# Hybrid decoder layer: late products by tile, and GpSimd's loads and sums behind copies

## The chip, the cores and the metric

The kernel runs on one core of one Trainium2 chip. The metric is the device time of one execution in microseconds (us); the number given for a kernel is the median of its runs.

## The reference

One decoder layer on 512 tokens with 16 learned meta tokens ahead (528 positions, 1024 channels), in float32:

```python
u = rmsnorm(h, mix_norm_w)
proj = u @ w_in                      # u_pool | z | xbc | dt | gates
gates = sigmoid(proj[..., OFF_GATE:] + b_gate)
y_pool = pool_mixer(u_pool, pool_w_group, pool_scale) @ w_pool_up
y_ssd = mamba2_branch(z, xbc, dt_raw, ...) @ w_ssd_out   # 8 groups, chunks of 128
h = h + (gate_pool * y_pool + gate_ssd * y_ssd) @ w_o
v = rmsnorm(h, mlp_norm_w)
hid = relu(v @ w_ff1)
h = h + (hid * hid) @ w_ff2
out = rmsnorm(h, final_norm_w)[:, N_META:]
```

`mamba2_branch` convolves xbc, scans chunk by chunk, adds a skip term, multiplies with silu(z) and normalizes each of the eight groups of 256 channels. `pool_mixer` takes running means over 2, 4, 8 and 16 positions in four groups and mixes each with a 256x256 matrix.

## The kernel before

Activations stand channels by tokens, 128 channels to a tile. Each float32 product is made of three matmuls of a faster type: a factor is cast to a high half (ScalarE: `whi`, `shi`, `yh`) and the rest is a low half (VectorE: `wlo`, `slo`, `yl`), and PE multiplies high by high, high by low and low by high. Many products are seven half-size ones in Strassen's way instead of eight; their factors need sums of quarters of the weights.

The stages follow each other: projections and scan of the groups 0 to 7, woven together; during the last group's scan, which has no projection beside it, `out_part` multiplies the scan's outputs with w_ssd_out; then the pool stage (`pool_pair`, `pool_mix`, and between them the last products of w_ssd_out, tiles psl); then the merge (`gate_ssd`, tiles pgs, and products with w_pool_up, tiles pup; the gates multiply, sums go to acc); then w_o (tiles wo_alpha, wo_q, wo_p); then the MLP, whose first layer's products (pf, px) run between those of the second (alpha, q, p).

**out_part.** The y of groups 0 to 6 are the 14 pairs `ys[0]` to `ys[13]`; this function uses 8 to 13. For the first two output tiles (psp0, psp1) it does `ys[8..11]` first, then, when the y of group 6 are there, the late products with `ys[12]` and `ys[13]`; then the six other tiles. Each tile is copied from PSUM by ScalarE (`add`, tile sp) and added to `acc_d` in DRAM by a GpSimd DMA. The PSUM pool psa has two buffers, so tile n + 2 waits for the copy of tile n. `ssd` of group 7 runs at the same time; at its end it makes the last y (`ys[14]`, `ys[15]`).

**Gates.** Seven pool gates lie in DRAM (`gate_d`) since the scan and are loaded into `m1[d]` by GpSimd DMAs in the pool stage; the eighth is written directly.

**Weight sums.** For each set of quarters in `sets`, `weight_sums` issues four (w_ff2) or eight (w_in, w_ff1) GpSimd DMAs of 512 KB that copy quarters from DRAM to DRAM and accumulate; the issuing queue waits where one step reads what another wrote. There are 15 sets, 11 of them are made in the scan, each step behind a copy of a column by GpSimd into `seen`, which makes it wait for its place. The remaining four are made at the end of the merge, behind the loads of `ht` (the residual), which wait until the memory of u is free:

```python
for t in range(4):
    ht_load = nc.gpsimd.dma_start(ht[:, t, :], x[t * P : (t + 1) * P, :])
while sets:
    with tc.issue_after(ht_load.ins):
        ht_load = weight_sums()
```

Weights come in blocks of 128 x 1024 (512 KB), loaded by SyncE into three `raw` buffers (`block_load`, L95); a load waits until VectorE has made the low half from the block before in that buffer. There are four buffers each for the halves.

The order of an engine's instructions is set by a scheduler from the order of the code and from estimates; `tc.issue_after(i)` puts an instruction behind another in its engine's order, `tc.high_priority` moves it ahead where its operands allow it. A DMA that stands behind a copy in GpSimd's queue waits for what that copy waits for.

Of the kernel before, what the change touches and what calls it, by code (L numbers as in the profile page):

```python
# [9 lines left out]
F32 = mybir.dt.float32  # L10
F32R = mybir.dt.float32r
AF = mybir.ActivationFunctionType
ALU = mybir.AluOpType

P = 128
# [37 lines left out]

SETS_AT = {0: 1, 1: 1, 2: 2, 3: 1, 4: 2, 5: 2, 6: 1, 7: 1}
PIECES = {4: 21, 7: 14}
SETS_POOL = 0

PLAIN = 4

# [5 lines left out]
def kernel(ctx: ExitStack, tc, xT, x, w, fx, f1, f2, vec, fnw, out):  # L65
# [100 lines left out]
    def col(off, i, n=P):  # L166
        return vs[:n, off + i : off + i + 1]
# [426 lines left out]
    def ssd(g, cur):  # L594
# [121 lines left out]
        for c in range(4):  # L716
            dve.reciprocal(rs[:, ctok(c)], rs[:, ctok(c)])
        yield
        for i in range(2):
            y = yt[:, i, :]  # L720
            dve.scalar_tensor_tensor(y, y, col(V_SN, 2 * g + i), rs, op0=ALU.mult, op1=ALU.mult)
            yh = yp.tile([P, SEQ], F32R, tag="yh", name=f"yh{g}_{i}")
            yl = yp.tile([P, SEQ], F32R, tag="yl", name=f"yl{g}_{i}")
            act.copy(yh, y)
            dve.tensor_tensor(yl, y, yh.bitcast(F32), op=ALU.subtract)
            ys.append((yh, yl))
        yield

    late_cast, last_state = [None], {}
# [112 lines left out]
    def out_part():  # L842

        def get(n):
            t = block_tiles()
            block_load(t, slice(0, 1024))

            with after(b_meta[G - 1] if n == 1 else None):
                cast = act.copy(t[2], t[1])
            if n == 1:  # L850
                late_cast[0] = cast
            with tc.issue_after(x_decayed[G - 1].ins) if n == 1 else nullcontext():
                dve.tensor_tensor(t[3], t[1], t[2].bitcast(F32), op=ALU.subtract)
            return t

        def pieces():
            blocks = [get(0), get(1)]
            for n in range(6):
                t = blocks[n] if n < 2 else get(n)
                for j in range(NK):  # L860
                    c = slice(j * P, (j + 1) * P)
                    yield t[2][:, c], t[3][:, c]

        un = pieces()

        def part(ps, d, ks):
            mm3s(ps, [(next(un), ys[k]) for k in ks], ks[0] == 8, ks[-1] == 13)

        def add(ps, d):
            o = staged(f"sp{d}")  # L870
            act.copy(o, ps)
            nc.gpsimd.dma_start(acc_d[d], o, accum_op=ALU.add)


        ps = [psum2(f"psp{d}")[:, :SEQ] for d in range(2)]
        for d in range(2):
            part(ps[d], d, range(8, 12))
            yield
        late = [[(next(un), ys[k]) for k in (12, 13)] for d in range(2)]
        for o in ((0, 0), (1, 0), (0, 1)):  # L880
            for d in range(2):
                for n, (a, b) in enumerate(late[d]):
                    pe.matmul(ps[d], a[o[0]], b[o[1]], start=False, stop=o[1] == 1 and n == 1)
            yield
        for d in range(2):
            add(ps[d], d)
        for d in range(2, NK):
            ps = psum2(f"psp{d}")[:, :SEQ]
            part(ps, d, range(8, 14))
            add(ps, d)  # L890
            yield
# [162 lines left out]

    for d in range(NK):
        t_load = nc.gpsimd.dma_start(acc[d], acc_d[d])
    for _ in range(SETS_POOL):
        with tc.issue_after(t_load.ins):
            t_load = weight_sums()
    pend = [pooled_halves(*a) for a in pool_pair(POOL_ORDER[0])]  # L1060

    un = units()
# [11 lines left out]
    for n in range(1, 4):  # L1074
        pend, ahead = nxt, None
        if n < 3:
            nxt, ahead = pool_pair(POOL_ORDER[n + 1]), POOL_ORDER[n + 1]
        if n == 2:
            wgb = block()
        else:  # L1080
            gts.append(gate_ssd(MERGE[len(gts)]))

        pend = [pooled_halves(*a, copied.get(ahead)) for a in pend]
        with tc.issue_after(last[ahead].ins) if n < 3 else nullcontext():
            pool_mix(POOL_ORDER[n], pend, wgb)
        if n == 1:
            for d in MERGE:
                with tc.issue_after(mixed[0].ins):
                    if d < NK - 1:
                        nc.gpsimd.dma_start(m1[d], gate_d[d])  # L1090
    pool_stack.close()
# [82 lines left out]
    for n, d in enumerate(MERGE):  # L1174

        with ExitStack() as st:
            if n == 1:
                for i in mixed:
                    st.enter_context(tc.issue_after(i.ins))
            if 0 < n < NK - 1:  # L1180
                gts.append(gate_ssd(MERGE[n + 1]))
        if n >= NK - 2:
            first.append(split(woq["b11", n - NK + 2]))
        ps = psum2(f"pup{d}")[:, :SEQ]
        wh, wl = block()
        if n < len(WO_ORDER):
            wo_load(*WO_ORDER[n])
        cs = [slice(k * P, (k + 1) * P) for k in ks]
        mm3s(ps, [((wh[:, c], wl[:, c]), yps[k]) for c, k in zip(cs, ks)])
        dve.tensor_tensor(acc[d], acc[d], gts[n], op=ALU.mult)  # L1190
        dve.tensor_tensor(m1[d], m1[d], ps, op=ALU.mult)
        dve.tensor_tensor(acc[d], acc[d], m1[d], op=ALU.add)
        factors(d)
# [652 lines left out]
```

## Time and profile before

| | |
|---|---|
| median of 3 runs | 1000.05 us (999.04 to 1002.26) |
| the profiled execution | 1001.71 us, span of its profile 1000.0 us |
| busy, share of the span | PE 99%, weight loads of PE 87%, DVE 80%, ACT 60%, POOL 12% |
| clock granted to TensorE | 0.998 |
| DMA | 184.52 MB, mean 185 GB/s |

PE is TensorE, PEld its weight loads, DVE VectorE, ACT ScalarE, POOL GpSimd, SP SyncE. In a timeline a row has the start in us, the busy time, the engine, the line, the operation, output<-inputs by tile names, shapes, the count, and in brackets the idle time before it with what ended it. Where one row holds several instructions, the busy time is that of all. Lines are those of the kernel before.

### The profile page before, as it was taken

The page shows a single profiled execution, that of the slowest core. Times are in us where ns is not written, and L with a number is a line of the kernel's source. Part 1 is how long each engine was busy: PE and PEld are TensorE (multiplying, and loading weights), DVE is VectorE, ACT ScalarE, POOL GpSimd, SP SyncE. Part 2 cuts the span into 40 slices and gives each one's busy share as a digit, 9 for nine tenths or more (in the row PEclk, how much of TensorE's full clock was granted, in tenths as well). Part 3 has the DMA queues.
Part 4 walks back from the last instruction along what each step waited for, and adds up shares of the span by engine and source line. Part 5 has one row for each costly group of instructions (what it writes and reads, how often), then busy time and mean ns, then how long its engine had stood idle before and what let it go on. Part 6 is the DMA issues. An engine that isn't in the chain of part 4 may idle for free.

```text
span 1000.0 us, 15672 instructions
## 1 busy us (share of the span) xinstructions
PE 987.8 (99%) x6035; PEld 873.8 (87%) x6035; DVE 803.9 (80%) x1162; ACT 602.2 (60%) x855; POOL 119.5 (12%) x215
## 2 busy tenths in 40 slices
PE   9999999999999999999999999999999999999997
PEld 7889998989889999978898888888789999999986
DVE  7978997879845888988789666975988888888885
ACT  7657839495924658574345433477666656656654
POOL 0011321211212212223200001121000000000000
PEclk9999999999999999999999999999999999999999
DMA  7284968666798848768723723899354454454332
GB/s 261 78 254 149 268 197 214 190 191 212 230 271 235 245 129 259 226 163 171 271 85 127 253 85 112 228 243 314 92 190 148 148 190 144 152 186 150 129 106 85
DMA packets 61803, 184.52 MB, mean 185 GB/s; under 512 B 7072, under 2 KB 8416, under 8 KB 60704
## 3 DMA queue, kind: packets, MB, share of 16 engines
q1 hardware_dynamic: 39456, 109.00, 32.7%
q0 software_dynamic: 18240, 67.51, 26.4%
q10 hardware_dynamic: 4032, 7.00, 1.9%
q8 instruction: 47, 0.77, 0.3%
q14 instruction: 28, 0.23, 0.1%
HBM read 173.13 MB, written 58.59 MB: 232 GB/s over the span
## 4 chain that ended last, share of the span: by engine, by line
PE 93%; ACT 3%; DVE 2%; DMA 1%; issue 0%; SPq 0%; ACTq 0%; DVEq 0%
PE px L1465 8%; PE px L215 8%; PE alpha L1533 6%; PE pz L215 6%; PE px L1468 4%; PE px L218 4%; PE alpha L1536 3%; PE pgp L215 3%; PE pz L218 3%; PE pgs L215 3%; PE py L694 2%; PE pqx L509 2%; PE pso L146 1%; PE pgp L218 1%; PE wo_alpha L1226 1%; PE po L688 1%
## 5 line engine op out<-in xcount | busy, mean ns | idle before, releaser
L113 DVE TENSOR_TENSOR wlo<-raw,whi 128x1024 fp32r<-128x1024 f32 (+2 forms) x88 | 102.0, 1171 | 46.8 <-ACT whi L111 31.0
L111 ACT CAST whi<-raw 128x1024 fp32r<-128x1024 f32 (+2 forms) x88 | 87.2, 1011 | 70.3 <-PE pso L147 15.3
L215 PE MATMUL px<-uh,whi 128*128 128x264 f32 (+1 forms) x320 | 80.9, 291 | 0.0
L218 PE MATMUL px<-ul,whi 128*128 128x264 f32 (+1 forms) x320 | 78.8, 285 | 0.0
L1240 DVE TENSOR_TENSOR ht<-ht,alpha 128x1024 f32<-128x1024 f32 x35 | 42.7, 1220 | 29.1 <-PE alpha L1533 29.1
L215 PEld LDWEIGHTS px<-uh,whi 128*128 128x128 f32 x320 | 60.4, 189 | 0.9 <-issue 0.7
L1162 ACT CAST shi<-rawf 128x1024 fp32r<-128x1024 f32 x42 | 44.2, 1053 | 28.0 <-PE alpha L1536 18.3
L218 PEld LDWEIGHTS px<-ul,whi 128*128 128x128 f32 x320 | 60.2, 188 | 0.4 <-issue 0.2
L1533 PE MATMUL alpha<-shi,hh 128*128 128x512 f32 x140 | 55.3, 395 | 2.0 <-DVE ht L1240 1.9
L1536 PE MATMUL alpha<-shi,hl 128*128 128x512 f32 x140 | 54.7, 391 | 0.0
L1163 DVE TENSOR_TENSOR slo<-rawf,shi 128x1024 fp32r<-128x1024 f32 x42 | 51.2, 1219 | 0.6 <-ACT shi L1162 0.6
L1468 PE MATMUL px<-vsl,shi 128*128 128x256 f32 x192 | 47.4, 280 | 0.0
L1465 PE MATMUL px<-vsh,shi 128*128 128x256 f32 x192 | 47.4, 281 | 0.0
L215 PE MATMUL pz<-uh,whi 128*128 128x512 f32 x112 | 43.7, 390 | 0.0
L218 PE MATMUL pz<-ul,whi 128*128 128x512 f32 x112 | 43.6, 389 | 0.0
L215 PE MATMUL px<-uh,wlo 128*128 128x264 f32 (+1 forms) x320 | 41.8, 283 | 0.0
L215 PEld LDWEIGHTS px<-uh,wlo 128*128 128x128 f32 x320 | 39.9, 188 | 0.0
L1533 PE MATMUL alpha<-slo,hh 128*128 128x512 f32 x140 | 37.4, 389 | 0.0
L1465 PEld LDWEIGHTS px<-vsh,shi 128*128 128x128 f32 x192 | 36.2, 188 | 0.9
L1468 PEld LDWEIGHTS px<-vsl,shi 128*128 128x128 f32 x192 | 36.1, 188 | 0.9
L1468 PE MATMUL px<-vl,shi 128*128 128x256 f32 x144 | 36.1, 283 | 0.0
L1465 PE MATMUL px<-vh,shi 128*128 128x256 f32 x144 | 36.0, 282 | 0.0
(599 smaller groups left out, 3064.8 us busy)
## 6 DMA issues: line engine op xcount, KB each, us to landing
raw<-in_w SPq DMA_DIRECT2D x96, 512.0 KB, 4.4
f_t<-in_f POOLq DMA_DIRECT2D x38, 512.0 KB, 7.4
f_s<-in_f POOLq DMA_DIRECT2D x26, 512.0 KB, 7.3
b<-in_f SPq DMA_DIRECT2D x21, 512.0 KB, 4.5
rawf<-in_f SPq DMA_DIRECT2D x36, 256.0 KB, 2.9
rawf<-f_t SPq DMA_DIRECT2D x36, 256.0 KB, 2.9
abc<-acs_d POOLq DMA_DIRECT2D x8, 1024.0 KB, 7.6
f_t<-f_t POOLq DMA_DIRECT2D x12, 512.0 KB, 6.7
```

The source lines that it names most:

```text
L111: act.copy(hi[:, c], raw[:, c])
L113: dve.tensor_tensor(lo[:, c], raw[:, c], hi[:, c].bitcast(F32), op=ALU.subtract)
L215: pe.matmul(o, wt, rhs[0][k][:, c], start=part == 0 and k == 0, stop=part == 1 and k == NK - 1)
L218: mm[0] = pe.matmul(o, wt, rhs[1][k][:, c], start=False, stop=False)
L509: at = pe.matmul(o, wk, f[k][0], start=start and not low and k == 0, stop=stop and low == 1 and k == 3, skip_group_check=True)
L1162: splits.append((act.copy(hi, src), dve.tensor_tensor(lo, src, hi.bitcast(F32), op=ALU.subtract)))
L1163: dve.tensor_tensor(lo, src, hi.bitcast(F32), op=ALU.subtract)))
L1240: added[0] = dve.tensor_tensor(o, o, src, op=op)
L1465: pe.matmul(ps, m, f[k][0], start=start and not low and k == 0, stop=stop and low == 1 and k == 3, skip_group_check=True)
L1468: pe.matmul(ps, m, f[k][1], start=False, stop=False, skip_group_check=True)
L1533: pe.matmul(ps[t], hh[:, p, seg, st], m, start=bool(first and not low and p == 0), stop=bool(last and low and p == 1), skip_group_check=True)
L1536: pe.matmul(ps[t], hl[:, p, seg, st], m, start=False, stop=False, skip_group_check=True)
```

## The change

Three things change. First, the late products of psp0 and psp1 are done tile by tile, not step by step over both; each tile's copy follows at once at high priority, and the making of the last y (group 7) gets the same priority. Second, the loads of the pool gates are put behind a GpSimd copy of a column of the first pool mix's output. Third, two of the four remaining weight sum sets are put behind a GpSimd copy of a column of the gate of merge step 3, ahead of the loads of ht.

```diff
@@ -53,7 +53,8 @@
 
 SETS_AT = {0: 1, 1: 1, 2: 2, 3: 1, 4: 2, 5: 2, 6: 1, 7: 1}
 PIECES = {4: 21, 7: 14}
-SETS_POOL = 0
+SUMS_BEHIND = 3
+SETS_MERGE = 2
 
 PLAIN = 4
 
@@ -716,14 +717,15 @@
         for c in range(4):
             dve.reciprocal(rs[:, ctok(c)], rs[:, ctok(c)])
         yield
-        for i in range(2):
-            y = yt[:, i, :]
-            dve.scalar_tensor_tensor(y, y, col(V_SN, 2 * g + i), rs, op0=ALU.mult, op1=ALU.mult)
-            yh = yp.tile([P, SEQ], F32R, tag="yh", name=f"yh{g}_{i}")
-            yl = yp.tile([P, SEQ], F32R, tag="yl", name=f"yl{g}_{i}")
-            act.copy(yh, y)
-            dve.tensor_tensor(yl, y, yh.bitcast(F32), op=ALU.subtract)
-            ys.append((yh, yl))
+        with tc.high_priority(100) if g == G - 1 else nullcontext():
+            for i in range(2):
+                y = yt[:, i, :]
+                dve.scalar_tensor_tensor(y, y, col(V_SN, 2 * g + i), rs, op0=ALU.mult, op1=ALU.mult)
+                yh = yp.tile([P, SEQ], F32R, tag="yh", name=f"yh{g}_{i}")
+                yl = yp.tile([P, SEQ], F32R, tag="yl", name=f"yl{g}_{i}")
+                act.copy(yh, y)
+                dve.tensor_tensor(yl, y, yh.bitcast(F32), op=ALU.subtract)
+                ys.append((yh, yl))
         yield
 
     late_cast, last_state = [None], {}
@@ -877,13 +879,13 @@
             part(ps[d], d, range(8, 12))
             yield
         late = [[(next(un), ys[k]) for k in (12, 13)] for d in range(2)]
-        for o in ((0, 0), (1, 0), (0, 1)):
-            for d in range(2):
+        for d in range(2):
+            for o in ((0, 0), (1, 0), (0, 1)):
                 for n, (a, b) in enumerate(late[d]):
                     pe.matmul(ps[d], a[o[0]], b[o[1]], start=False, stop=o[1] == 1 and n == 1)
+            with tc.high_priority(100):
+                add(ps[d], d)
             yield
-        for d in range(2):
-            add(ps[d], d)
         for d in range(2, NK):
             ps = psum2(f"psp{d}")[:, :SEQ]
             part(ps, d, range(8, 14))
@@ -1054,9 +1056,6 @@
 
     for d in range(NK):
         t_load = nc.gpsimd.dma_start(acc[d], acc_d[d])
-    for _ in range(SETS_POOL):
-        with tc.issue_after(t_load.ins):
-            t_load = weight_sums()
     pend = [pooled_halves(*a) for a in pool_pair(POOL_ORDER[0])]
 
     un = units()
@@ -1084,8 +1083,9 @@
         with tc.issue_after(last[ahead].ins) if n < 3 else nullcontext():
             pool_mix(POOL_ORDER[n], pend, wgb)
         if n == 1:
+            at = pool.tensor_copy(seen, yps[2 * POOL_ORDER[0]][0].bitcast(F32)[:, :1])
             for d in MERGE:
-                with tc.issue_after(mixed[0].ins):
+                with tc.issue_after(at.ins):
                     if d < NK - 1:
                         nc.gpsimd.dma_start(m1[d], gate_d[d])
     pool_stack.close()
@@ -1179,6 +1179,11 @@
                     st.enter_context(tc.issue_after(i.ins))
             if 0 < n < NK - 1:
                 gts.append(gate_ssd(MERGE[n + 1]))
+        if n == SUMS_BEHIND:
+            put = pool.tensor_copy(seen, gts[n][:, :1])
+            for _ in range(SETS_MERGE):
+                with tc.issue_after(put.ins):
+                    put = weight_sums()
         if n >= NK - 2:
             first.append(split(woq["b11", n - NK + 2]))
         ps = psum2(f"pup{d}")[:, :SEQ]
```

The instructions stand in another order on three engines. The following rows are the order of the instructions in the program, without times. Names carry numbers: psp0 is the first tile, yh6_0 and yl6_0 the halves of `ys[12]`, whi57 and wlo57 those of weight block 57, st0_7 a state of the scan. Lines of the changed kernel are one to five higher.

TensorE at the late products, before, from the second step of psp1:

```order
L883 MATMUL psp1_4665<-yh6_0_4624,whi57_4673 128x512
L883 MATMUL psp1_4665<-yh6_1_4629,whi57_4673 128x512
L883 MATMUL psp0_4664<-yh6_0_4624,wlo57_4674 128x512
L883 MATMUL psp0_4664<-yh6_1_4629,wlo57_4674 128x512
L688 MATMUL po7_0_4756<-ct7_4163,st0_7_4730 128x128
L883 MATMUL psp1_4665<-yh6_0_4624,wlo57_4674 128x512
L883 MATMUL psp1_4665<-yh6_1_4629,wlo57_4674 128x512
L883 MATMUL psp0_4664<-yl6_0_4625,whi57_4673 128x512
L883 MATMUL psp0_4664<-yl6_1_4630,whi57_4673 128x512
L883 MATMUL psp1_4665<-yl6_0_4625,whi57_4673 128x512
L883 MATMUL psp1_4665<-yl6_1_4630,whi57_4673 128x512
L146 MATMUL psp2_4817<-yh4_0_3552,whi57_4673 128x512
```

and now, from the third matmul of psp0:

```order
L885 MATMUL psp0_4664<-yh6_0_4624,wlo57_4674 128x512
L885 MATMUL psp0_4664<-yh6_1_4629,wlo57_4674 128x512
L885 MATMUL psp0_4664<-yl6_0_4625,whi57_4673 128x512
L885 MATMUL psp0_4664<-yl6_1_4630,whi57_4673 128x512
L689 MATMUL po7_0_4761<-ct7_4163,st0_7_4730 128x128
L885 MATMUL psp1_4665<-yh6_0_4624,whi57_4673 128x512
L885 MATMUL psp1_4665<-yh6_1_4629,whi57_4673 128x512
L885 MATMUL psp1_4665<-yh6_0_4624,wlo57_4674 128x512
L885 MATMUL psp1_4665<-yh6_1_4629,wlo57_4674 128x512
L885 MATMUL psp1_4665<-yl6_0_4625,whi57_4673 128x512
L885 MATMUL psp1_4665<-yl6_1_4630,whi57_4673 128x512
L147 MATMUL psp2_4808<-yh4_0_3552,whi57_4673 128x512
```

The matmuls are the same; those of psp0 now end before those of psp1 begin.

ScalarE at the same place, before (sp0 and sp1 are the copies, abc7 the decays of group 7):

```order
L670 COPY st0_7_4730<-pst7_0_4734 128x256
L647 ACTIVATE abc7_4633<-abc7_4633 128x1024
L849 CAST whi58_4819<-raw58_4818 128x1024
L648 ACTIVATE abc7_4633<-abc7_4633 128x1024
L871 COPY sp0_4811<-psp0_4664 128x512
L871 COPY sp1_4814<-psp1_4665 128x512
L849 CAST whi59_4888<-raw59_4887 128x1024
L849 CAST whi60_4916<-raw60_4915 128x1024
```

and now:

```order
L671 COPY st0_7_4730<-pst7_0_4734 128x256
L648 ACTIVATE abc7_4633<-abc7_4633 128x1024
L873 COPY sp0_4757<-psp0_4664 128x512
L649 ACTIVATE abc7_4633<-abc7_4633 128x1024
L873 COPY sp1_4785<-psp1_4665 128x512
L851 CAST whi58_4810<-raw58_4809 128x1024
L851 CAST whi59_4878<-raw59_4877 128x1024
L851 CAST whi60_4916<-raw60_4915 128x1024
```

The copy of psp0 moved ahead of the second decay and both copies ahead of the cast of block 58.

ScalarE at the end of the products and in the first pool pair, before (yh7 are the casts of the last y, whiS3 that of a sum of weights, pu the pool pair's outputs from pxx and pz):

```order
L724 CAST yh7_0_4877<-yt7_4755 128x512
L724 CAST yh7_1_4882<-yt7_4755 128x512
L871 COPY sp6_4967<-psp6_4942 128x512
L132 CAST whiS3_5039<-sm3_5032 128x1024
L132 CAST whiD3_5045<-raw62_5028 128x1024
L132 CAST whiB3_5049<-raw63_5030 128x512
L871 COPY sp7_4989<-psp7_4970 128x512
L1011 COPY pu6_5053<-pxx3_5055 128x264
L111 CAST whi64_5177<-raw64_5176 128x1024
L1017 ACTIVATE pu7_5054<-pxx3_5055 128x264
L111 CAST whi65_5215<-raw65_5214 128x1024
L1020 COPY pu7_5054<-pz3_5057 128x264
```

and now:

```order
L873 COPY sp6_4967<-psp6_4942 128x512
L726 CAST yh7_0_4905<-yt7_4760 128x512
L726 CAST yh7_1_4910<-yt7_4760 128x512
L133 CAST whiS3_5039<-sm3_5032 128x1024
L873 COPY sp7_4989<-psp7_4970 128x512
L133 CAST whiD3_5045<-raw62_5028 128x1024
L1013 COPY pu6_5053<-pxx3_5055 128x264
L133 CAST whiB3_5049<-raw63_5030 128x512
L112 CAST whi64_5177<-raw64_5176 128x1024
L1019 ACTIVATE pu7_5054<-pxx3_5055 128x264
L1022 COPY pu7_5054<-pz3_5057 128x264
L112 CAST whi65_5215<-raw65_5214 128x1024
```

The copy of tile 6 moved ahead of yh7, and that of pz (pu7) ahead of the cast of block 65.

GpSimd's queue, before (f14 is set 4 of w_ff1, f25 set 5 of w_ff2):

```order
L1090 DMA m1_2_5000<-gate_d2_137 128x512
L1090 DMA m1_6_5004<-gate_d6_141 128x512
L1090 DMA m1_3_5001<-gate_d3_138 128x512
L1202 DMA ht_6454<-in_x 128x1024 x4
L777 DMA f14_t1_504<-in_f1 128x1024
L778 DMA f14_s3_505<-in_f1 128x1024
L781 DMA f14_t2_506<-in_f1 128x1024
L779 DMA f14_t1_504<-in_f1 128x1024
```

and now:

```order
L1090 DMA m1_3_5001<-gate_d3_138 128x512
L1183 COPY seen_89<-gs5_6039 128x1
L779 DMA f14_t1_504<-in_f1 128x1024
L780 DMA f14_s3_505<-in_f1 128x1024
L783 DMA f14_t2_506<-in_f1 128x1024
L781 DMA f14_t1_504<-in_f1 128x1024
L784 DMA f14_s3_505<-in_f1 128x1024
L787 DMA f14_t4_507<-in_f1 128x1024
L786 DMA f14_t2_506<-f14_t1_504 128x1024
L788 DMA f14_t4_507<-f14_t2_506 128x1024
L779 DMA f25_t1_508<-in_f2 128x1024
L780 DMA f25_s3_509<-in_f2 128x1024
```

Behind the gate loads there is a new copy, and the sets f14 and f25 follow it; the ht loads come behind f25, and then the last two sets.

## The prediction

> **What bounds the kernel now.** I read the page's busy times first, then PE's own waits, then the timelines around each of them, and last the DMA at the places where the waits come from. The first row is the page's list of busy time by engine:
>
> ```profile
> PE 987.8 (99%) x6035; PEld 873.8 (87%) x6035; DVE 803.9 (80%) x1162; ACT 602.2 (60%) x855; POOL 119.5 (12%) x215
> ```
>
> TensorE is the bound and almost gapless. This change removes no matmul, so it can only win what PE still waits. The view of waits, for PE alone, begins with the longest (who waited, line, for whom: total us, times, longest us):
>
> ```profile
> PE alpha L1533 <- DVE ht L1240: 1.9, 1, 1.9
> PE pdt L260 <- DVE ones_r L157: 1.5, 1, 1.5
> PE psp L146 <- ACT sp L871: 1.5, 1, 1.5
> ```
>
> The middle one is the start of the kernel and stays. The other two are single stalls, and a third, small one follows below. An idle of x costs x + 0.16 us: a 512-column matmul is busy 0.39 us but the next starts after 0.23, as these PE rows of the timeline show (start, busy, ... x4: four take 1.07, and (1.07 - 0.39)/3 = 0.23):
>
> ```profile
> 722.19 0.39 PE L147 MATMUL pf<-vl,whi 128*128 128x512 f32 x1
> 722.41 1.07 PE L149 MATMUL pf<-vh,wlo 128*128 128x512 f32 x4
> 725.37 0.47 PE L1533 MATMUL alpha<-shi,hh 128*128 128x512 f32 x1 [1.89 <-DVE ht L1240]
> ```
>
> So the stalls are worth 1.89 + 0.16 = 2.05 and 1.46 + 0.16 = 1.62 us. The whole purse is about 4 us of 1000.
>
> **Part 1, the late products.** PE's timeline where the second stall lies, and then ScalarE's beside it:
>
> ```profile
> 441.54 1.07 PE L883 MATMUL psp<-yl,whi 128*128 128x512 f32 x4
> 444.07 0.50 PE L146 MATMUL psp<-yh,whi 128*128 128x512 f32 x1 [1.46 <-ACT sp L871]
> ```
>
> ```profile
> 440.60 1.06 ACT L647 ACTIVATE abc<-abc 128x1024 f32<-128x1024 f32 x1
> 441.55 1.04 ACT L849 CAST whi<-raw 128x1024 fp32r<-128x1024 f32 x1
> 442.49 1.05 ACT L648 ACTIVATE abc<-abc 128x1024 f32<-128x1024 f32 x1
> 443.45 1.05 ACT L871 COPY sp<-psp 128x512 f32<-128x512 f32 x2
> ```
>
> The third output tile needs one of the two PSUM buffers, so its first matmul waits for the copy of tile 0, which stands on ScalarE behind a decay, a weight cast and a second decay. PE is through with all twelve late matmuls at 441.54 + 4 x 0.23 = 442.45. The last six of them are now tile 1's, so tile 0 is complete by 442.45 - 6 x 0.23 = 441.1. Its copy now stands right behind the first decay: 441.6 to 442.1. That is 0.3 us before PE wants the buffer, so the 1.62 us go. No instruction is added. What the copies push back is the cast of block 58, from 441.55 to 443.6 (second decay to 443.1, second copy to 443.6), done at 444.6. PE uses that block after eight more matmuls (442.45 + 8 x 0.23 = 444.3) and after two dozen small ones of the scan, which at 128 columns take some 2 us together (an estimate from 0.23 for 512, doubled for the short ones); that is the cover. Bounds: nothing at all if another operand is late, and the full 1.62; I take the full value, since each time in this chain comes from a row.
>
> **Part 1, what comes late behind it.** On ScalarE the copy of tile 4 now stands ahead of the cast of the last squares (L330), and that of tile 6 ahead of the casts of the last y (L724). The first is hidden by the second, since those casts wait for tile 6 anyhow. ScalarE and VectorE in before, at the end of these products:
>
> ```profile
> 466.54 1.28 ACT L724 CAST yh<-yt 128x512 fp32r<-128x512 f32 x2
> 470.02 0.59 ACT L871 COPY sp<-psp 128x512 f32<-128x512 f32 x1 [2.20 <-PE psp L149]
> ...
> 475.51 0.38 ACT L1011 COPY pu<-pxx 128x264 f32<-128x264 f32 x1 [0.83 <-PE pxx L1004]
> ```
>
> ```profile
> 467.19 1.36 DVE L725 TENSOR_TENSOR yl<-yt,yh 128x512 fp32r<-128x512 f32 x2
> 468.46 0.69 DVE L985 TENSOR_TENSOR sm<-raw,raw 128x512 f32<-128x512 f32 x1
> ```
>
> The copy of tile 6 is tied to PE and moves up by 1.62: 468.4 to 469.0. Behind it come the two yh casts (1.28): 470.2. The second yl ends about 0.7 later (468.55 against 467.82 in before): 470.9. Two additions of 0.69 make the block sum sm: 472.3. Its cast (1.05, as the cast row above) ends at 473.3, the copy of tile 7 (0.59) at 473.9, the next cast at 474.8 and the copy of pxx (0.38, once at 475.51) at 475.2. PE gets to the product that overwrites pxx, which starts at 476.75 in the next fence, 1.62 earlier: 475.13. So all slack here is used up; stalls of 0 to about 1 us are possible, and I take 0.1 us.
>
> The third stall lies in this same pool pair, on PE and ACT:
>
> ```profile
> 476.75 0.28 PE L1004 MATMUL pxx<-t0h,whiS 128*128 128x264 f32 x1
> ...
> 481.57 0.39 PE L1004 MATMUL pz<-t1h,whiB 128*128 128x264 f32 x1 [0.26 <-ACT pu L1020]
> ```
>
> ```profile
> 480.19 1.05 ACT L111 CAST whi<-raw 128x1024 fp32r<-128x1024 f32 x1 [1.39 <-DMA raw<-in_w]
> 481.14 0.37 ACT L1020 COPY pu<-pz 128x264 f32<-128x264 f32 x1
> ```
>
> The copy of pz waited behind a weight cast that waited for its load. In the new order of ScalarE the copy stands ahead of that cast, so the 0.26 + 0.16 = 0.42 us go. PE uses the block of that cast only after two more products and the first four tiles of the next stage (24 matmuls x 0.23 = 5.4 us), which cover it.
>
> **Part 2, the gate loads.** The first GpSimd copy makes seven loads wait for the first of the four pool mixes, instead of following the loads of acc. They are read first here, on VectorE, in the merge stage behind the whole pool stage:
>
> ```profile
> 558.96 0.69 DVE L1191 TENSOR_TENSOR m<-m,pup 128x512 f32<-128x512 f32 x1 [0.29 <-PE pup L149]
> ```
>
> Three pool mixes lie between, so the wait costs nothing. Behind the copy on GpSimd's queue stand only those loads and then the sums. The weight loads of the first pool pair lose a competitor; I count no gain for it, as PE does not wait for them once the order of ScalarE is changed. If the loads came so late that this multiplication waited, PE would feel it through the merge's PSUM buffers; I give that no price.
>
> **Part 3, the two sum sets.** This is where the largest stall comes from. ScalarE, VectorE and the windows (busy us of PE, PEld, DVE, ACT, POOL, then clock, DMA share, GB/s):
>
> ```profile
> 686.24 1.05 ACT L111 CAST whi<-raw 128x1024 fp32r<-128x1024 f32 x1 [4.04 <-DMA raw<-in_w]
> ```
>
> ```profile
> 687.33 1.23 DVE L113 TENSOR_TENSOR wlo<-raw,whi 128x1024 fp32r<-128x1024 f32 x1 [5.40 <-ACT whi L111]
> ...
> 724.01 1.22 DVE L1240 TENSOR_TENSOR ht<-ht,alpha 128x1024 f32<-128x1024 f32 x1
> ```
>
> ```profile
> 680.00:700.00 20.00, 20.00 (x90) 16.54 (x89) 10.82 (x15) 14.14 (x20) 3.53 (x5) 1.00 1.00 305
> 700.00:724.00 24.00, 23.48 (x104) 19.13 (x102) 23.70 (x38) 14.10 (x21) 0.00 (x0) 1.00 0.34 81
> ```
>
> The DMA engines are full until 700. One weight load lands late, ScalarE stands 4.04 us for it, VectorE 5.40 us behind that, and VectorE then works off the debt without a gap (23.70 of 24 us) until its addition of alpha at 724.01, for which PE waits. What fills the DMA are the weight sums; GpSimd's queue:
>
> ```profile
> 619.06 1.58 POOL L1202 DMA_DIRECT2D ht<-in_x  x3 [130.90 <-PE pgs L215]
> ...
> 656.75 0.83 POOL L777 DMA_DIRECT2D f_t<-in_f  x1
> ...
> 697.79 0.82 POOL L782 DMA_DIRECT2D f_s<-in_f  x1 [0.76 <-DMA f_s<-in_f]
> ```
>
> All four sets start behind the ht loads: two from about 621 (619.06 and four issues) to 656.75, two from there to the last issue at 697.79. Two of them now start behind this gate, 45 us earlier:
>
> ```profile
> 575.50 0.68 ACT L1052 ACTIVATE gs<-pgs,vs 128x512 f32<-128x512 f32 x1
> ```
>
> At the old pace (35 us for two sets) they are issued by about 611, before the ht loads are let go at 619 (617 now), so ht is not delayed. The other two sets then take the place of the first two, 619 to about 656, and from about 665 the weight loads have the DMA to themselves. The load at 686 then lands before ScalarE asks for it at 682.2, and the DVE chain starts up to 4.04 us earlier against PE. PE gets to the product that needs alpha at 722.41 + 4 x 0.23 = 723.3, so the addition, done at 725.2, must be 1.9 us earlier to save the whole stall. It can start no sooner than the product it adds has ended; behind that product PE does twelve pf matmuls, of which the last four start at 722.41, so it ends near 722.41 - 8 x 0.23 + 0.2 = 720.8, or 3.2 us before 724.01. Since 4.04 and 3.2 are both above 1.9, I take the full 2.05; zero is the lower bound, if the debt is mostly VectorE's own work and comes back, and 2.05 the upper, as PE has no more to lose there.
>
> What the sets cost where they go is the landing of weight loads, first between 575 and 620 (issues: KB each, median us to landing), then between 660 and 700:
>
> ```profile
> raw<-in_w SPq DMA_DIRECT2D x6, 512.0 KB, 3.4
> ```
>
> ```profile
> DMA to landing us min/median/max: 3.8/9.7/13.0
> ```
>
> The second row is what the sums do to the same loads. In the merge stage PE uses a block in 24 x 0.227 = 5.44 us and three loads are in flight, so a load may take 3 x 5.44 = 16.3 us before the ring falls behind. 13.0 is less. I count nothing, with the far end priced as a rival.
>
> The Trainium skill (DMA: Bandwidth & Descriptors, "Issuing engines are not separate DMA queues") says that DMAs of all issuing engines run on the same 16 engines and interleave. By that rule alone the collision would only move to the merge stage, and the sum would keep the scan's part alone, about -2 us; the 3.4 against 9.7 us above speaks for room in the merge stage, so here I go by the rows.
>
> **The sum.** 1.62 + 0.42 - 0.1 + 2.05 = 4.0 us. The profiled execution took 1001.71 us with a span of 1000.0; the median of the runs is 1000.05, which is 1.7 below it. I subtract from the median: 996.0 us.
>
> **The rivals.**
> *A, only the scan wins* (chance 0.20): VectorE's debt is its own, or that load stays late behind other weight loads. For it: VectorE is busy 23.70 of 24 us, and the quarters of the MLP's weights are loaded at the same time as that block. Against it: it sat idle 5.40 us just before. 1000.05 - 1.94 = 998.1.
> *B, the last y takes the scan's gain back* (0.12): by the chain above there is no slack left at 475, and each us by which ScalarE is later is a us of PE. It decides when ScalarE is more than 0.1 us later than worked out; at 2 us the scan's part is gone: 1000.05 - 2.05 = 998.0.
> *C, slower* (0.10): the sums starve the merge stage. The mechanism is the ring of three weight buffers; it decides at landings over 16.3 us. At 20 us a block takes 6.67 instead of 5.44, and the 35 us of sums hold some seven blocks: +8.6 us; with the last stall and the scan's gain off, 1000.05 + 8.6 - 4.0 = 1004.6. For it: loads and sums together gave up to 13.0. Against it: no load in any row is near 16, and between 575 and 620 there are only six weight loads in 45 us.
> *D, nothing moves* (0.08): each freed us turns into a wait a few us later, because VectorE (80%) and PE are both close to full: 1000.
>
> **How the numbers follow.** My forecast has 0.50 and gives 995.0 to 997.0, as the -0.1 and the 2.05 vary; a measurement of this kernel can tell some 0.3%, 3 us, from no change, which puts the line for faster at 997.05. Nearly all of the forecast's cases and a few of A and B lie below it: faster 0.51. A, B and D lie within: 0.38. C and a little more: slower 0.11. The range takes in the forecast, A and B with half a us to a us of spread on either side: 994.9 to 999.3.
>
> **What would show it.** Right: PE's wait on the sp copy, on the pu copy and on alpha are gone from its list; no ACT wait for a raw load near 680; the DMA share at 680 to 700 well under 1.00 and that at 580 to 600 higher than in before; GpSimd idle after about 660. Wrong: a PE wait on a pu or whiS operand near 475 (B), a PE or ACT wait on raw loads between 575 and 615 (C), VectorE still gapless from 700 and PE still waiting for alpha (A).

## The result and the profile after

The changed kernel takes 1003.70 us (median of 9 runs, 1003.00 to 1006.43) against 1000.05 of before; the ratio is 1.0034, with a 95% interval of 1.0025 to 1.0043. In the rounds of later runs it was 1.0031 (1.0019 to 1.0043). The forecast was 996.0 us, so it is wrong in sign: slower by some 3.5 us, outside the range. The profiled execution took 1006.43 us with a span of 1004.7, the longest of its nine; what it shows is checked below against a second profile of 1002.97.

The longest waits of PE in it (who waited, line, for whom: total us, times, longest):

```profile
PE psl L147 <- DVE acc L1066: 3.7, 2, 2.0
PE psl L147 <- DVE pu L1028: 1.7, 1, 1.7
...
PE pxx L1006 <- ACT pu L1013: 1.3, 1, 1.3
PE pxx L1006 <- ACT pu L1019: 0.9, 1, 0.9
```

The three waits that the prediction wanted gone (for the sp copy, for the pu copy of pz, for alpha) are gone. PE's rows at two of those places carry no idle time in brackets any more, and the windows ahead of the product alpha, in the MLP (busy us of PE, PEld, DVE, ACT, POOL, then clock, DMA share, GB/s) show a DMA that is far from full and a VectorE with a little air:

```profile
442.08 0.39 PE L147 MATMUL psp<-yh,whi 128*128 128x512 f32 x1
...
724.89 0.39 PE L1538 MATMUL alpha<-shi,hh 128*128 128x512 f32 x1
```

```profile
680.00:700.00 20.00, 20.00 (x92) 16.55 (x91) 13.29 (x26) 16.75 (x26) 0.00 (x0) 1.00 0.56 195
700.00:724.00 24.00, 24.00 (x108) 19.87 (x107) 23.05 (x36) 15.71 (x22) 0.00 (x0) 1.00 0.14 45
```

Five new stalls stand against that, three in the stage that fills the psl tiles (the last y's products) and two in the next pool pairs. In the rows below their idle times add up to 1.67 + 1.97 + 1.70 + 1.30 + 0.88 = 7.5 us; each costs a little more than its length, and small gaps come with them. The whole account comes from setting the starts of the same matmuls of both traces side by side: PE loses 6.6 us in the psl stage and 3.1 in the pool pairs, and wins 2.3 from the late products to the end of the first pool pair and 2.3 at alpha. It was 0.4 us ahead of before when it reached the late products, and all this together is the 4.7 us between the spans (1004.7 and 1000.0).

**The first place.** ScalarE, then VectorE of the changed kernel (start, busy, ..., idle before it and its releaser in brackets):

```profile
467.86 0.59 ACT L873 COPY sp<-psp 128x512 f32<-128x512 f32 x1 [3.54 <-PE psp L150]
468.34 1.14 ACT L726 CAST yh<-yt 128x512 fp32r<-128x512 f32 x2
471.66 1.05 ACT L133 CAST whiS<-sm 128x1024 fp32r<-128x1024 f32 x1 [2.17 <-DVE sm L989]
472.61 0.58 ACT L873 COPY sp<-psp 128x512 f32<-128x512 f32 x1
473.09 1.05 ACT L133 CAST whiD<-raw 128x1024 fp32r<-128x1024 f32 x1
...
485.12 1.05 ACT L112 CAST whi<-raw 128x1024 fp32r<-128x1024 f32 x1 [7.01 <-DMA raw<-in_w]
```

```profile
474.17 1.23 DVE L134 TENSOR_TENSOR wloD<-raw,whiD 128x1024 fp32r<-128x1024 f32 x1 [0.20 <-ACT whiD L133]
...
486.21 1.23 DVE L114 TENSOR_TENSOR wlo<-raw,whi 128x1024 fp32r<-128x1024 f32 x1 [6.52 <-ACT whi L112]
487.35 0.42 DVE L1028 TENSOR_TENSOR pu<-pu,pz 128x264 f32<-128x264 f32 x1
...
490.64 0.68 DVE L1066 TENSOR_TENSOR acc<-acc,psl 128x512 f32<-128x512 f32 x1
```

The same cast of D and its low half in before, and the DMA issues of SyncE in before and after:

```profile
471.46 1.04 ACT L132 CAST whiD<-raw 128x1024 fp32r<-128x1024 f32 x1
...
472.73 1.22 DVE L133 TENSOR_TENSOR wloD<-raw,whiD 128x1024 fp32r<-128x1024 f32 x1
```

```profile
473.98 5.16 SPq L95 DMA_DIRECT2D raw<-in_w  x3
```

```profile
475.42 2.40 SPq L96 DMA_DIRECT2D raw<-in_w  x3
```

The chain reads: the copy of tile 6 stands ahead of the last y's casts (yh at 468.34, in before 466.54), and the copy of tile 7 ahead of the cast of D (473.09, in before 471.46). VectorE's low half of D is the last reader of that raw buffer, so the load of a later weight block (block 65), which goes into that buffer, is issued at 475.42 and not 473.98; as this execution was 0.4 us ahead of before at 440, the lag is rather 1.8. The load lands at 485.12 and not 480.19. ScalarE stands 7.01 us for it, VectorE 6.52 behind ScalarE; and on VectorE, which takes its queue in order, the addition of pz (L1028) and all additions of psl into acc stand behind that low half. They give back the PSUM tiles that PE needs:

```profile
487.83 0.50 PE L147 MATMUL psl<-yh,whi 128*128 128x512 f32 x1 [1.67 <-DVE pu L1028]
...
491.46 0.47 PE L147 MATMUL psl<-yh,whi 128*128 128x512 f32 x1 [1.97 <-DVE acc L1066]
...
497.88 0.50 PE L147 MATMUL psl<-yh,whi 128*128 128x512 f32 x1 [1.70 <-DVE acc L1066]
```

**The second place.** GpSimd's queue, VectorE, and PE in the next pool pairs:

```profile
507.13 0.18 POOL L1086 COPY seen<-yph 128x1 f32<-128x1 f32 x1 [28.09 <-ACT yph L1045]
507.36 2.12 POOL L1090 DMA_DIRECT2D m<-gate_d  x4
509.80 1.75 POOL L1090 DMA_DIRECT2D m<-gate_d  x3 [0.32 <-issue]
```

```profile
518.91 0.69 DVE L987 TENSOR_TENSOR sm<-raw,raw 128x512 f32<-128x512 f32 x1 [3.18 <-DMA raw<-in_w]
```

```profile
522.10 0.39 PE L1006 MATMUL pxx<-t0h,whiS 128*128 128x264 f32 x1 [1.30 <-ACT pu L1013]
...
526.17 0.39 PE L1006 MATMUL pxx<-t0h,whiD 128*128 128x264 f32 x1 [0.88 <-ACT pu L1019]
```

The seven gate loads now go out just when the weight blocks of the following pool pair are on their way; VectorE waits 3.18 us for one of those blocks; in before the same addition (L985, at 511.76) waits for none.

### The profile page after: what moved, and what is told of

Same layout as the page of the kernel before. It is cut to its first block, busy times and chain, and to the rows that moved or that the text cites. A ratio compares the mean times of both kernels' runs of the same rounds, so it can differ in the third digit from the quotient of the medians.

```text
span 1004.7 us, 15676 instructions
## 1 busy us (share of the span) xinstructions
PE 988.6 (98%) x6035; PEld 872.7 (87%) x6035; DVE 803.6 (80%) x1162; ACT 601.5 (60%) x855; POOL 120.1 (12%) x217
## 4 chain that ended last, share of the span: by engine, by line
PE 91%; DVE 3%; ACT 3%; DMA 2%; issue 1%; SPq 0%; ACTq 0%; DVEq 0%
PE px L1470 8%; PE px L216 8%; PE alpha L1538 6%; PE pz L216 6%; PE px L1473 4%; PE px L219 4%; PE alpha L1541 3%; PE pgp L216 3%; PE pz L219 3%; PE pgs L216 3%; DMA raw<-in_w 2%; PE pqx L510 2%; PE py L695 2%; PE po L689 2%; PE pso L147 1%; PE pgp L219 1%
```

## The theories

**T1, a chain of buffers.** The late products shift ScalarE's order, the raw buffer of D comes back late, block 65 lands late, VectorE stands in order, psl stalls. **T2, the gate loads.** At their new place they collide with the weight loads of the second pool pair. **T3, the sums** starve the merge stage (rival C of the prediction). **T4**, added during the work: the earlier accumulating copies and the loads of acc crowd the DMA, whatever ScalarE's order.

The high priority that the change puts on the last y moves nothing: with it and without it all five engines have the same instructions in the same order, so it wasn't run by itself. The medians of before differ a little between the groups of runs (1000.1 to 1001.5 us), so kernels are compared by their ratios to before in the same group.

## The parts one by one

**e1: the late products and the last y alone** (gate loads and sums as in before).

> Only the late products with early copies and the last y (gate loads and sums as in before). T1, the order of ScalarE and VectorE: the last y's casts come 1.8 us later behind the copy of tile 6, block 65's raw buffer is given back late, its load bunches with two others, and VectorE stands in order at that block's low half ahead of the adds that free the psl PSUM tiles; PE loses about 6 us in the psl stage and wins 2.0 before it: 1000 + 4 = about 1004, with psl stalls of over 1 us each. T2, the moved gate loads do it: without them no psl stall, 998 to 999.

Measured: 1002.63 us, ratio 1.0016 (1.0006 to 1.0025). The psl stalls are there without the gate loads' move:

```profile
PE psl L147 <- DVE acc L1066: 3.6, 2, 1.9
```

Matmul by matmul beside before, PE wins 2.3 us up to 482 and loses 4.7 from there to 500. (The span of its profile is 1000.2 us all the same, as this execution has no wait for alpha; see the sums' term below.) T1 holds as to the place; I had the size too high (6), since the third stall, on the addition of pz, isn't there. In the second profile of the whole change it isn't either: block 65 lands at 483.5 and 482.9 in these two and at 485.1 in the first.

**e2: the gate loads alone.**

> Only the gate loads moved behind the first pool mix's column. T1 (the order does it): the psl stage as in before, total within 1 us of 1000. T2 (the gate loads collide with the weight loads of the second pool pair at 507 to 520 us): PE waits about 1.3 and 0.9 us for pu copies near 520 to 525, total 1002 to 1003.

Measured: 1003.67 us, ratio 1.0025 (1.0014 to 1.0036). The psl stage is as in before; VectorE and PE in the pool pairs:

```profile
514.40 0.69 DVE L986 TENSOR_TENSOR sm<-raw,raw 128x512 f32<-128x512 f32 x1 [2.16 <-DMA raw<-in_w]
```

```profile
517.59 0.39 PE L1005 MATMUL pxx<-t0h,whiS 128*128 128x264 f32 x1 [0.28 <-ACT pu L1012]
521.66 0.39 PE L1005 MATMUL pxx<-t0h,whiD 128*128 128x264 f32 x1 [0.86 <-ACT pu L1018]
```

The weight loads of this stretch take longer to land (before, then e2, both from 500 to 525; KB each, median us from issue to landing):

```profile
raw<-in_w SPq DMA_DIRECT2D x5, 512.0 KB, 3.8
```

```profile
raw<-in_w SPq DMA_DIRECT2D x4, 512.0 KB, 5.7
```

The first wait is smaller than the 1.3 that I expected. Matmul by matmul, PE loses 2.1 us here, about what the ratio says. So there are two losses, each there without the other. Net of the gains this one is the larger by the medians, but the two intervals overlap.

**e3: the two sum sets alone**, and **e4: late products and sums** (the whole change without the move of the gate loads).

> Only the two sum sets moved behind the gate's column. T1 and T2 alike: no wait for alpha near 723, nothing lost in the merge, 998.0 (before less 2.05). T3 (the sums starve a stage): PE waits for weight casts between 575 and 620, over 1000.

> The whole change without the move of the gate loads. T1: the loss in the psl stage stays, alpha's wait is gone: about 1002 (e1 less 2), and 1.5 us or so under the whole change at most. T2: the losses are gone, 996 to 997.

Measured: e3 1000.52 us, ratio 0.9992 (0.9982 to 1.0002); e4 1002.37 us, ratio 1.0015 (1.0006 to 1.0024). No wait of PE appears in the merge stage, and the weight loads between 575 and 620 land in 6.0 and 6.2 us (median; 3.4 in before), 7.6 at most, so T3 falls. The ratios add up: +0.16, +0.25 and -0.08% make +0.33, for +0.34 and +0.31 of the whole. But the sums bring 0.8 us, with an interval that includes nothing, and not 2.05; that is taken up at the end of the experiments.

## Mending the late products

**e5: the copy of tile 6 behind the last y's casts**, the rest as in e1:

```diff
-            act.copy(o, ps)
+            with tc.issue_after(last_yh[-1].ins) if d == 6 else nullcontext():
+                act.copy(o, ps)
```

> The late products alone, as in the first experiment, with the copy of tile 6 held behind the casts of the last y on ScalarE. T1 as a chain of buffers: this lifts only the first link; the copy of tile 7, which waits for PE until about 472.5, still stands ahead of the cast of D, so that cast starts near 473.1 and not 473.45, the raw buffer comes back at most 0.4 us earlier, and the psl stalls stay: about 1002. A looser form of T1 (only the last y's lateness counts): psl stalls gone, about 999.

Measured: 1002.28 us, ratio 1.0012 (1.0001 to 1.0023). ScalarE and VectorE:

```profile
473.07 0.58 ACT L875 COPY sp<-psp 128x512 f32<-128x512 f32 x1 [1.08 <-PE psp L150]
473.55 1.05 ACT L133 CAST whiD<-raw 128x1024 fp32r<-128x1024 f32 x1
```

```profile
474.64 1.22 DVE L134 TENSOR_TENSOR wloD<-raw,whiD 128x1024 fp32r<-128x1024 f32 x1 [1.38 <-ACT whiD L133]
```

ScalarE now idles 1.08 us at the copy of tile 7, with the cast of D behind it. The low half of D starts at 474.64, at 474.53 in e1; as PE in this execution runs 0.8 us behind that of e1 already at 440, that is some 0.7 us earlier than in e1 and still 1.1 later than in before. PE still stalls for psl tiles, 1.4 and 1.7 us. The looser form of T1 falls, the chain stands: it has two links on ScalarE, and the lateness of y is only the first.

**e6: the copies of tile 7 and of pxx behind the casts of S, D and B as well.** The copy of tile 7 is written after the pool pair's casts and waits for the cast of B (as does the first pu copy); the loads of acc are written behind the pool pair too. The main lines:

```diff
+        for add, ps in put_off:
+            with tc.issue_after(fb_cast.ins):
+                add(ps, NK - 1)
```

> The late products alone, with ScalarE's order of before restored from the last y on: copy of tile 6 behind the casts of y, copy of tile 7 and the copy of pxx behind the casts of S, D and B. T1: the raw buffers come back as early as before or earlier, no psl stall, the gain of 1.6 to 2.0 us is kept: about 999. Rival T4 (the earlier accumulating copies and loads of acc crowd the DMA, whatever ScalarE's order): psl stalls of over 1 us stay, 1002.

Measured: 1000.87 us, ratio 0.9995 (0.9982 to 1.0008). The stalls on acc are gone, but one is new, on the addition of pxx, which on VectorE stands behind the low half of block 65:

```profile
PE pxx L1018 <- DVE pu L1037: 2.4, 1, 2.4
```

So the result lies between T1's and T4's: the old stalls went, as T1 said, but one of over 1 us is there in another place, and the load of that block is still what decides. This profile is the longest of the twelve runs (1003.20 us), and behind the stall its matmuls run at half the clock for 3.4 us (last section). **e8** is this kernel with the gate loads mended (e7, next section) and the sums.

> All three parts, with ScalarE's order of before from the last y on and the gate loads behind the second mix. T1 and T2 together: the losses of both parts go and the gains of the late products (1.6 to 2.0) and of the sums (0.4 to 2.0) stay: 997 to 999. If either theory is wrong: 1001 or more.

Measured: 999.38 us, ratio 0.9979 (0.9967 to 0.9992): faster than before, with the stall on the addition of pxx left:

```profile
482.93 0.39 PE L1018 MATMUL pxx<-uh,whiD 128*128 128x264 f32 x1 [1.68 <-DVE pu L1037]
```

**e9: VectorE alone.** ScalarE's order as the change leaves it, the low half of block 65 behind the addition of pz:

```diff
-            hi, lo = block()
+            hi, lo = block(next(behind, None))
...
-    un = units()
+    un = units((None, pz_add[0]))
```

> The late products alone, with ScalarE as the change leaves it, and one edit on VectorE: the low half of block 65 stands behind the addition of pz (which frees the PSUM that the pool pair ends on) instead of ahead of it. T1's last link, VectorE in order: the load of 65 still lands near 483, but the adds that give the psl PSUM back no longer wait for it; the psl stalls of 2.1 and 1.8 us go, PE wants the block itself only near 487: about 999, ratio to before near 0.998. T4 (DMA crowding or ScalarE's order is enough by itself): stalls remain in the psl stage, now on the block's halves, 1002.

Measured: 1002.75 us, ratio 1.0019 (1.0010 to 1.0029): no gain at all. PE and VectorE:

```profile
488.38 0.47 PE L150 MATMUL psl<-yh,whi 128*128 128x512 f32 x1 [0.37 <-DVE acc L1069]
494.78 0.50 PE L150 MATMUL psl<-yh,whi 128*128 128x512 f32 x1 [2.07 <-DVE acc L1069]
```

```profile
485.05 1.22 DVE L114 TENSOR_TENSOR wlo<-raw,whi 128x1024 fp32r<-128x1024 f32 x1 [3.48 <-ACT whi L112]
...
490.56 2.36 DVE L114 TENSOR_TENSOR wlo<-raw,whi 128x1024 fp32r<-128x1024 f32 x2
...
494.04 0.68 DVE L1069 TENSOR_TENSOR acc<-acc,psl 128x512 f32<-128x512 f32 x1
```

My claim that VectorE's order is the link to cut falls. VectorE still idles 3.48 us for the late block, has its averages left to do afterwards, and the debt comes out at the fourth addition of acc, behind the next two low halves: the first stall shrinks, the second grows. This profile, too, is the longest of its twelve runs (1005.51 us), with half the clock behind the second stall (last section); how much of the edit's gain is lost to that in the other runs isn't known.

**e10: both** (e8 with the edit of e9), and **e11: the whole change with only two edits**, the gate loads' later place and the edit of e9, ScalarE's order left as the change has it.

> All parts, ScalarE's order of before, the gate loads behind the second mix, and the low half of block 65 behind the addition of pz. T1: the last stall of the mended version (1.8 us on the addition of pxx, which stands behind that low half) goes as well: 1.5 us under the mended version, ratio to before near 0.996. T4: no better than the mended version, 0.998.

> The whole change with two edits only: the gate loads behind the second mix, the low half of block 65 behind the addition of pz; ScalarE's order as the change leaves it. T1 and T2: both losses go, the same as the previous one or up to 1 us more, ratio 0.996 to 0.997. If ScalarE's order costs by itself (late casts of D and B): 0.998 to 1.000.

Measured: e10 997.86 us, ratio 0.9970 (0.9958 to 0.9982); e11 1000.69 us, ratio 0.9998 (0.9988 to 1.0007). ScalarE and VectorE of e10:

```profile
471.80 1.05 ACT L135 CAST whiD<-raw 128x1024 fp32r<-128x1024 f32 x1 [0.15 <-DVE raw L1002]
...
480.47 1.05 ACT L112 CAST whi<-raw 128x1024 fp32r<-128x1024 f32 x1 [1.55 <-DMA raw<-in_w]
```

```profile
481.80 1.22 DVE L114 TENSOR_TENSOR wlo<-raw,whi 128x1024 fp32r<-128x1024 f32 x1
```

Block 65 lands at 480.47 and VectorE doesn't wait for it; PE has no gap of 0.2 us or more left behind the late products. e10 and e11 differ by 0.28%, 2.8 us. What separates them is ScalarE's order and what it takes along: in e10 two loads of acc stand ahead of the store of tile 7 on GpSimd, and on VectorE the low half of B ahead of the addition of py. VectorE's order is worth something only once the block is nearly on time: the stall of 1.68 us in e8 is gone in e10, though the two ratios are not clear of each other. T4 as it was put, whatever ScalarE's order, falls, as the same copies and loads are in e10. But they aren't at the same times (the last load of acc is issued at 484.30 in e10, at 478.44 in e12), so a part of the DMA traffic in block 65's shorter flight is not excluded.

## The gate loads' place, and the sums

**e7: the gate loads behind the second pool mix**, nothing else:

```diff
-            at = pool.tensor_copy(seen, yps[2 * POOL_ORDER[0]][0].bitcast(F32)[:, :1])
+            at = pool.tensor_copy(seen, yps[2 * POOL_ORDER[1]][0].bitcast(F32)[:, :1])
```

> Only the gate loads moved, but behind the second pool mix instead of the first: issued near 532 us, where the trace of before shows a DMA share of 0.00 from 529 to 537. T2 (they cost by colliding with the second pair's weight loads): no wait of PE between 517 and 523, the same as before within 0.5 us: 1000.4 to 1001.4. Rival: moving them costs as such, 1003.

Measured: 1001.39 us, ratio 1.0002 (0.9991 to 1.0014). GpSimd of e7, and the window 529 to 537 in before and in e7:

```profile
531.96 3.75 POOL L1089 DMA_DIRECT2D m<-gate_d  x7
```

```profile
529.00:537.00 8.00, 8.00 (x55) 7.42 (x55) 7.89 (x13) 4.96 (x8) 0.00 (x0) 1.00 0.00 0
```

```profile
529.00:537.00 8.00, 8.00 (x58) 7.53 (x57) 7.82 (x12) 5.34 (x9) 4.46 (x8) 1.00 0.46 151
```

The same seven loads, 25 us later, in a stretch where the DMA was idle, cost nothing: T2 holds, it is the place and not the move. **e14** has them where before has them, in the otherwise mended kernel:

> The mended version with the gate loads where before has them (480 to 490 us, together with the loads of acc and of the next weight blocks). If their going helps the landing of block 65: 0.5 to 1.5 us over the mended version, and a stall behind that load near 482. If it doesn't: the same.

Measured: 997.28 us, ratio 0.9962 (0.9950 to 0.9974), no slower than e10. Block 65 lands 1.0 us later after its issue than in e10 (482.22 from 474.86, against 480.47 from 474.14), but PE doesn't notice. So the move of the gate loads had nothing to win; this kernel, without it, has the lowest ratio of all, though not clear of that of e10.

**The sums' term.** e13 is e10 without the move of the sums, e15 and e16 are before once more; e12 is the whole change again.

> The mended version with all three edits, without the move of the two sum sets. If the wait for alpha (1.9 us in the profiled execution of before) is there in each execution: 2 us over the mended version, ratio 0.999. If it comes and goes from execution to execution, as the traces so far suggest: 0.5 to 1 us over it, ratio 0.9975 to 0.998, and a wider spread of its runs.

> The kernel before, unchanged, one more profile. Stall fixed: a wait of about 1.9 us for alpha near 725 and a load that ScalarE waits 4 us for near 682. Stall not fixed: the wait is absent or of another size.

> The same once more: with the profiles of the kernels that leave the sums in place, this shows in how many executions the wait for alpha is there.

> The whole change once more, on the chip and in the rounds of the mended ones: ratio 1.003 to 1.004; a profile to see whether the third psl stall of 1.8 us (on the addition of pz) is there every time or hangs on when the load of block 65 lands.

e13: 998.34 us, ratio 0.9967 (0.9954 to 0.9980), not to be told from e10. e12: 1004.00 us, ratio 1.0031 (1.0019 to 1.0043), without the third psl stall. PE's wait for alpha in e13, e15 and e16:

```profile
PE alpha L1548 <- DVE ht L1255: 0.8, 1, 0.8
```

```profile
PE alpha L1533 <- DVE ht L1240: 0.4, 1, 0.4
```

```profile
PE alpha L1533 <- DVE ht L1240: 0.6, 1, 0.6
```

Ten profiles of kernels with the sums at their old place show this wait as 1.9 (before), 0.4 and 0.6 (before again), 0 (e1), 1.5 (e2), 0, 0, 0 (e5, e6, e7), 2.6 (e9) and 0.8 (e13): 0.78 on average. All eight profiles with the sums moved show none. In all ten the DMA share from 680 to 700 is 1.00 or more, and the three longest stalls (before, e2, e9) go with the three latest landings of the load that ScalarE waits for there (686.24, 688.38 and 689.99; the others 675.65 to 685.64). So the traces bear the mechanism out, and the stall is of another size in each execution. 0.8 us is what the median of e3 gave, too, but neither e3's interval nor e13 beside e10 tells it from nothing.

## Why the prediction was wrong, point by point

- **Part 1, the stalls for the sp and the pu copy (1.62 + 0.42): right.** Both are gone, and the mended kernel keeps the gain; matmul by matmul it is 1.8 + 0.5 us.
- **Part 1, "what comes late behind it" (0.1 us): this step failed.** The chain itself was right and even cautious: I had the cast of D done at 474.8, it was done at 474.14, and the product that overwrites pxx did not wait, just as worked out. But I followed it only to the next matmul that reads PSUM. I did not follow the low half of D to the buffer it frees and from there to the load of block 65, of which I wrote that 24 matmuls, 5.4 us, cover it. For PE itself they nearly did: in the first profile it began the four tiles at 481.89 and would have wanted the block at 487.3, and the low half was done at 487.44. VectorE, however, stands in its queue for that block with the PSUM-freeing additions behind. Measured in e1: 3.6 us of stalls, 4.7 us of PE's time, instead of 0.1.
- **Rival B had the place, not the price.** It said that ScalarE has no slack left at 475 and priced that at 2 us, the scan's gain. It decides through the ring of weight buffers, which gives back more than the lateness. In e1, whose PE is level with that of before at 440, the load of block 65 is issued 1.8 us later and lands 3.3 us later; in the first profile after, 1.44 us at the issue became 4.9 at the landing.
- **Part 2, "the wait costs nothing": failed.** I looked at who reads the gate loads (at 559) and who is relieved where they leave, and never at what they meet where they arrive. The cost is 2.5 us (e2), nothing at 532 (e7), nothing where they were (e14).
- **Part 3 (2.05): right in the mechanism, too large by some 1.2 us.** It took one profile's stall for that of every execution.
- **Rival C** (the sums starve the merge stage), which carried the chance of a slower kernel, did not happen; the landings between 575 and 620 took 8.5 us at most in the kernels with the sums moved, below its 16.3 us point as argued. The slower side came from two mechanisms that had no price.

The forecast of 996 was thus the time of another kernel: e14, with the two losses undone, has 0.9962 of before, 3.8 us less. That it comes so near is partly chance: its late products win 2.3 us where the forecast had 1.9, its sums some 0.8 where the forecast had 2.05, and its interval is 1.2 us to either side.

## What to carry to other kernels

When a step comes later on an engine, follow the buffer it frees to the load that waits for it, and that load to everything that stands in order behind its first reader; PE's own need of the data is only one of the ends. A transfer that is moved must be looked at where it arrives: list the loads in flight there before calling it free. And a stall that hangs on a DMA's landing should be read from several profiles before it goes into a sum at full size.

## What the runs showed of the hardware

In some executions a stall of about 2 us was followed by matmuls at half the clock. Windows of e4 (as above; the clock is the column ahead of the DMA share), and PE behind the stall:

```profile
488.00:490.00 2.00, 0.46 (x3) 0.04 (x1) 1.93 (x4) 1.32 (x2) 0.00 (x0) 1.00 1.02 383
490.00:492.00 2.00, 1.59 (x4) 1.33 (x5) 2.00 (x5) 0.00 (x0) 0.00 (x0) 0.63 0.59 234
492.00:494.00 2.00, 2.00 (x6) 1.52 (x6) 2.00 (x4) 0.75 (x1) 0.00 (x0) 0.52 0.01 4
```

```profile
490.41 0.67 PE L147 MATMUL psl<-yh,whi 128*128 128x512 f32 x1 [1.95 <-DVE acc L1066]
```

For 3.4 us the matmuls start 0.43 us apart instead of 0.23, which adds 8 x 0.2 = 1.6 us to that stall. The same stands in e9 and e11 behind stalls of 2.1 us and in e6 behind one of 2.4 (clock 0.50 from 486 to 488), but not in e1 and the first profile after behind stalls of 1.95 and 1.97, nor in e9 behind its wait of 2.56 us for alpha. The Trainium skill (TensorE: Matmul & The Clock Gate, "HAM oscillation — how this bites in real kernels") puts the abstract rule as no idle gaps of PE over some 3.4 us; here gaps of 2 us sufficed in some executions, so a short stall's price isn't its own length. What makes the one execution throttle and the other not stays open.

Open, too, is why the load of block 65 flies longer in the changed kernels. Over all 18 traces its flight, from the issue to the cast that waits for it, goes with how close together the three raw loads are issued. Where the row of the three issues takes 5.16 us, as in before, the flight is 5.7 to 6.5 us (before three times, e2, e3, e7); where it takes 3.6 us, it is 6.3 to 7.4 (e6, e8, e10, e13, e14); where it takes 2.4 to 2.6 us, it is 7.4 to 9.7 (the change twice, e1, e4, e5, e9, e11). In the middle group the longest two, 7.2 and 7.4, are those with gate loads issued near 477 (e6, e14). No run moved one of these alone.
